# Another offset for a few split weight pages in a stream of three-pass fp32 matmuls

## The chip, the cores and the metric

The kernel runs on one core of one Trainium2 chip. The metric is the device time of one execution in microseconds; of several runs the median is taken.

## What is computed

One layer of a hybrid encoder over 512 tokens of width 2048, all in fp32. Cut to what matters:

```python
h = rms_norm(x, norm_mix_w)
q_a, k_a, v_a, q_g, k_g, v_g, r_g, gate_lr = split(h @ w_in)
y_a = chunked_band_attention(q_a, k_a, v_a, bias)      # 16 heads of 64
o_g = gated_linear_attention(q_g, k_g, v_g, log_a)     # 4 heads
y_g = rms_norm(o_g, gla_norm_w) * silu(r_g)
x = x + concat(y_a, y_g) @ w_out                       # 2048 x 2048
h = rms_norm(x, norm_ffn_w)
u_gate, u_val = split(conv3(h @ w_ffn_up))             # 2048 x 11264
x = x + (gelu(u_gate) * u_val) @ w_ffn_down            # 5632 x 2048
h = rms_norm(x, norm_ple_w)
x = x + sigmoid(h @ w_ple_gate) * (p @ w_ple_proj)     # 2048 x 2048
return rms_norm(x, final_norm_w)
```

## The kernel before

**Products.** The large projections are done by a Strassen-like scheme: a unit is two output blocks of 128 for all 512 tokens, and it is made of seven products (`PLAIN`: P1, P2, P6, P5, P7, P3, P4) of a sum of weight blocks with a prepared combination of the activations. A product is one step. fp32 accuracy comes from splitting each operand into a high and a low part in the matmul's rounded fp32 type: `product` runs three passes over the blocks of 128 of the inner dimension, (high weights, high activations), (high, low), (low, high). With eight blocks (`kb` = 8) a step is 24 matmuls of 128x128 weights with 256 moving columns, with seven blocks 21. The activations are the moving operand; the weight page is the one that is loaded into the array.

**Stages.** The steps lie in one list, `steps`, of 704. `base` says at which step a unit begins. The stages in order: front (16 units: 4 for the linear attention, 8 for the attention, then 4 gate units, 112 steps), the embedding (4 steps of another form), `wo` (8 units, 56 steps), `up` (44 units, 308 steps), `dn0` (8 units, 56 steps, eight blocks), `dn1` and `dn2` (56 steps each, seven blocks), `pg` (56 steps). From `wo` on, the first two and the last two units of a stage are paired: their products alternate, 14 steps for the two.

**Weight pages.** Raw weights come by DMA into pages; some are summed, by a DMA that accumulates (GpSimd's queue) or by VectorE. Two steps before a step's matmuls, `prep_high` has ScalarE write the page's high part (`w<-l` or `w<-s` in the profile) and `prep_low` has VectorE write the low part. Both go into one tile, `w_all`, of 6280 columns: three places for high parts at 0, 1024 and 2048 plus a shift, and three for low parts 3136 columns further on. `weight_pages(shift)` hands them out in rotation, so that step i uses the place of step i-3. In the main loop the shift is 24 columns, so each page starts 96 bytes past a multiple of 256. The tile itself starts at a multiple of 256 in the core's memory, as the compiled program of this kernel places it, and the tiles of the activations (`h`, `wo_R`, `up_N` and the like) start 32 bytes past one; so a page starts 64 bytes further on than its moving operand, modulo 256. For the value projections at the start, where the page is the moving operand and 512 columns are streamed at a time, the shift is 72 (32 bytes past a multiple of 256), and 24 for the last two pages (`value_split`). The last three steps of all put their pages into a free activation tile named `last` (32 bytes past a multiple of 256), as no place of the rotation is free.

**Order.** The order of the engines' work is written out by hand: an `agenda` lists for every step the copies, sums and stores to be issued with it. The three normalisations between stages come as small matmuls in the stage after them (`norm_step`: tile `ms` at the 11th step, `pb` at the 13th).

```python
def weight_pages(shift=72):
    i = counts.get("w", 0)
    counts["w"] = i + 1
    o = i % 3 * 1024 + shift
    return w_all[:, o:o + 1024], w_all[:, 3136 + o:4160 + o]
```

The functions that the change touches:

Of the kernel before, what the change touches and what calls it, by code (L numbers as in the profile page):

```python
# [42 lines left out]
def encoder_block(ctx: ExitStack, tc: tile.TileContext, A, out):  # L43
# [81 lines left out]
# [5 lines that stand above are left out]
# [349 lines left out]
    def make(unit, name):  # L479
        if name not in unit.made:  # L480
            return
        unit.made.discard(name)
        n = unit.stage.kb * P
        w = lambda q: unit.w[q][:, :n]
        if name == "S1":
            vec.tensor_tensor(made_page(unit, "S1")[:, :n], w("L21"), w("L22"), ALU.add)
            used(unit, "L21")
            used(unit, "L22")
            if unit.sums == "s3":
                unit.made.discard("S3")  # L490
                nc.gpsimd.dma_start(w("L21"), w("L11"), accum_op=ALU.add)
                used(unit, "L11")
        elif name == "S2":
            make(unit, "S1")
            vec.tensor_tensor(made_page(unit, "S2")[:, :n], w("S1"), w("L11"), ALU.add)
            used(unit, "S1")
            used(unit, "L11")
        elif name == "S3":
            make(unit, "S1")
            if "S3" in unit.made or unit.sums == "dve":  # L500
                vec.tensor_tensor(w("L21"), w("L21"), w("L11"), ALU.add)
                used(unit, "L11")
        else:
            vec.tensor_tensor(w("S2"), w("S2"), w("L12"), ALU.add)
            used(unit, "L12")

    def prep(i, own=None):
        prep_low(prep_high(i, own))

    def prep_high(i, own=None):  # L510
        if i >= len(steps):
            return None
        unit, prod = steps[i]
        name = PRODUCTS[prod][0]
        n = unit.stage.kb * P
        make(unit, name)
        if prod == unit.order[0] and unit.sums in ("dve", "s3"):
            make(unit, "S1")
        if i + 1 < len(steps):
            nxt, p = steps[i + 1]  # L520
            q = PRODUCTS[p][0]
            if (nxt is unit or nxt.paired) and (q != "S4" or "P6" in nxt.w) and (unit, q) != (front.units[6], "S2"):
                make(nxt, q)
        if i > 0 and steps[i - 1][1] == "P6" and steps[i - 1][0].paired:
            make(steps[i - 1][0], "S4")
        key = name
        if unit.sums != "memory":
            key = {"S4": "S2"}.get(name, "L21" if name == "S3" and unit.sums != "dma" else name)
        raw = unit.w[key]
        hi, lo = own or weight_pages(24)  # L530
        act.activation(hi[:, :n], raw[:, :n], AF.Copy)
        unit.w[prod] = hi, lo
        return unit, key, hi[:, :n], lo[:, :n], raw[:, :n]
# [66 lines left out]
    def load_x(src, unit):  # L600
        unit.xs = page("c", "xs").rearrange("p (s t) -> p s t", s=2)
        nc.sync.dma_start(unit.xs, src[unit.u])
# [56 lines left out]
    def after_norm(dst, xd, col):  # L659
        def after(unit):  # L660
            if unit.last is not None:
                return [(1, 0, lambda: nc.sync.dma_start(dst[unit.u], unit.xs))] + squares(unit, 6 + unit.last * 2)
            return [(0, 1, lambda: residual(dst, unit)), (1, 2, lambda: weighted(col, unit)),
                    (2, 1, lambda: store_pair(xd, unit.u, unit.o[:, 0, :], unit.o[:, 1, :]))] + squares(unit, 3)
        return after
# [46 lines left out]
    def after_gate(unit):  # L712
# [9 lines left out]
    stages = [Stage("wo", list(range(8)), 8, mixd, blk2(A["w_out"]), after_norm(streams[1], h2d, nffn), "s3", "dma", ends=("memory", None),  # L722
                    begin=lambda u: load_x(streams[0], u), begin_at=10, chained=True)]
# [165 lines left out]
    def front_weights(u, q):  # L889
# [4 lines left out]
    front = Stage("in", [12, 13, 14, 15] + list(range(12)), 8, None, front_weights,  # L894
                  lambda u: (attend if u.u < 8 else after_gates if u.u < 12 else linear)(u), "dma",
                  "dma", single=True, late={-4: 6, -12: 3, -11: 2, -10: 1})
# [20 lines left out]
    base = {}  # L917
    for st in stages:
        for group in st.groups:
            base[group[0]] = base[group[-1]] = len(steps)  # L920
            steps += [(u, p) for p in group[0].order for u in group]
            for u in group:
                u.paired = len(group) > 1
            need = [[(u, name) for name in (NEEDS[u.sums] if u.stage is not embed else ("L11",))] for u in group]
            wanted += [e for es in zip(*need) for e in es]

    agenda = [[] for _ in range(len(steps) + 60)]
    now = [0]
    for a, b in zip(stages[2:], stages[3:]):
        i0 = base[a.units[-1]]  # L930
        for n, p in enumerate(PLAIN):
            op = PRODUCTS[p][1]
            for g in range(2):
# [3 lines left out]
                at = 2 * n + (11 if g else 8)  # L937
                k = 3
                if g and b.chained and op in ("R21", "T4"):
                    at, k = max(at, 15), 0 if op == "R21" else 3  # L940
                if b.chained and op == "N1":
                    at = 17 + g
# [109 lines left out]
    for n in range(2):  # L1052
        u = stages[-1].units[n - 2]
        at = end + 4 + n
# [503 lines left out]
    for i, (unit, prod) in enumerate(steps[:-4]):  # L1558
        st = unit.stage
# [7 lines left out]
        if not behind:  # L1567
            coming = prep_high(i + 2) if i < len(steps) - 5 else None
# [3 lines left out]
        if behind:  # L1572
            coming = prep_high(i + 2)
# [112 lines left out]
    lo, hi = lo_half, hi_half  # L1686
# [133 lines left out]
```

## Time and profile before

| | |
|---|---|
| median of 3 runs | 2240.18 us (2231.03 to 2240.95) |
| profiled execution, its own time | 2243.69 us |
| its span, first to last instruction | 2241.9 us |
| mean granted TensorE clock | 0.997 |
| TensorE (PE) busy | 2217.4 us, 18248 matmuls |
| VectorE (DVE) busy | 1895.9 us |
| ScalarE (ACT) busy | 1320.6 us |
| HBM over the span | 273 GB/s |

PE is TensorE's matmuls, PEld its weight loads, which overlap them. A matmul of 256 columns is recorded as lasting about 0.28 us from its first operand to its last result, but the next begins long before it ends; so the busy time of PE says little, and what counts is the time from one start to the next. A stretch of time (a window) lists how many instructions touch it; since a matmul that only reaches into it counts too, a long window has two or three too many.

### The profile page before, as it was taken

What the parts mean: (1) busy time and instruction counts of PE and PEld (TensorE: products, weight loads), DVE (VectorE), ACT (ScalarE), POOL (GpSimd) and SP (SyncE); (2) the same over time, 40 slices, a digit from 0 to 9 for tenths busy, and PEclk for the clock granted to TensorE, in tenths of its full rate; (3) what the DMA queues carried; (4) which work ended last, traced back from release to release, by engine and by line L of the source; (5) the groups of instructions that cost most, each with busy time, mean ns of one, the idle gap of its engine ahead of it and who ended that gap; (6) DMA issues with size and microseconds to landing.
All of it is one profiled execution on the core that took longest, in us unless ns stands there. A gap on an engine that the chain in (4) does not pass through costs nothing.

```text
span 2241.9 us, 45663 instructions
## 1 busy us (share of the span) xinstructions
PE 2217.4 (99%) x18248; PEld 2167.5 (97%) x18248; DVE 1895.9 (85%) x2601; ACT 1320.6 (59%) x1960; POOL 201.0 (9%) x245
## 2 busy tenths in 40 slices
PE   9999999999999999999999999999999999999997
PEld 8879999999899999999999999999999999999997
DVE  6876779997698989898888888888888798898997
ACT  6654567776665765555555545555564564666765
POOL 1021111011100011111111100000000000000000
PEclk9999999999999999999999999999999999999999
DMA  5498889888978979999999987877876967879896
GB/s 206 139 260 246 227 232 250 227 229 236 352 270 250 348 212 286 284 273 288 281 271 275 264 230 207 218 210 193 246 266 221 300 231 231 333 248 333 286 299 207
DMA packets 202340, 569.77 MB, mean 254 GB/s; under 512 B 22064, under 2 KB 64304, under 8 KB 202128
## 3 DMA queue, kind: packets, MB, share of 16 engines
q1 hardware_dynamic: 168336, 448.58, 56.2%
q0 software_dynamic: 32352, 115.88, 27.4%
q8 instruction: 143, 2.34, 0.4%
q10 hardware_dynamic: 1440, 2.40, 0.3%
q14 instruction: 69, 0.57, 0.1%
HBM read 493.37 MB, written 119.54 MB: 273 GB/s over the span
## 4 chain that ended last, share of the span: by engine, by line
PE 81%; DVE 7%; DMA 7%; ACT 2%; issue 2%; SPq 0%; DVEq 0%; POOL 0%; ACTq 0%; POOLq 0%
PE accA L64 41%; PE accC L64 21%; PE accB L64 10%; PE v L64 4%; DVE w L64 2%; DMA on<-ond 1%; DMA s<-in_w_blk 1%; PE pp L64 1%; DMA l<-in_w_ple_gate 1%; DMA wva_s<-in_w_v_a 1%; PE psc L64 1%; PE py L64 1%; PE ptr L64 1%; ACT w L64 1%; DVE u L64 1%
## 5 line engine op out<-in xcount | busy, mean ns | idle before, releaser
L64 PE MATMUL accA<-h,w 128*128 128x256 f32 x5088 | 623.4, 280 | 1.7 <-ACT u L64 1.2
L64 PEld LDWEIGHTS accA<-h,w 128*128 128x128 f32 x5088 | 604.1, 189 | 4.7 <-ACT u L64 2.1
L64 PE MATMUL accC<-h,w 128*128 128x256 f32 x4248 | 520.9, 280 | 3.6 <-DVE w L64 2.6
L64 DVE TENSOR_TENSOR w<-s,w 128x1024 fp32r<-128x1024 f32 (+1 forms) x381 | 457.4, 1201 | 73.7 <-ACT w L64 71.6
L64 PEld LDWEIGHTS accC<-h,w 128*128 128x128 f32 x4248 | 504.9, 189 | 4.5 <-DVE w L64 3.0
L64 ACT ACTIVATE w<-l 128x1024 fp32r<-128x1024 f32 (+1 forms) x320 | 331.7, 1038 | 183.4 <-PE accC L64 119.5
L64 DVE TENSOR_TENSOR w<-l,w 128x1024 fp32r<-128x1024 f32 (+1 forms) x320 | 382.4, 1195 | 58.8 <-ACT w L64 58.6
L64 ACT ACTIVATE w<-s 128x1024 fp32r<-128x1024 f32 (+1 forms) x381 | 394.7, 1037 | 41.2 <-DVE s L64 26.6
L64 ACT ACTIVATE u<-accA 128x256 f32<-128x256 f32 x302 | 114.2, 378 | 376.4 <-PE accA L64 375.7
L64 DVE TENSOR_TENSOR s<-s,l 128x1024 f32<-128x1024 f32 (+1 forms) x176 | 211.3, 1201 | 8.5 <-DMA s<-in_w_blk 8.1
L64 POOL DMA_DIRECT2D s<-in_w_up x84 | 73.9, 880 | 743.8 <-DMA s<-in_w_up 326.2
L64 DVE SCALAR_TENSOR_TENSOR cv<-u,cw,cv 128x511 f32<-128x511 f32 (+1 forms) x176 | 131.6, 748 | 3.1
L64 PE MATMUL accA<-up_R,w 128*128 128x256 f32 x1056 | 131.5, 281 | 0.0
L64 PE MATMUL accB<-up_R,w 128*128 128x256 f32 x1056 | 131.1, 281 | 0.0
L64 PE MATMUL accA<-up_N,w 128*128 128x256 f32 x1056 | 131.1, 281 | 0.0
L64 PEld LDWEIGHTS accA<-up_R,w 128*128 128x128 f32 x1056 | 127.2, 189 | 0.5 <-issue 0.5
L64 PEld LDWEIGHTS accB<-up_R,w 128*128 128x128 f32 x1056 | 127.2, 189 | 0.0
L64 PEld LDWEIGHTS accA<-up_N,w 128*128 128x128 f32 x1056 | 127.1, 189 | 0.0
L64 DVE TENSOR_TENSOR u<-u,accC 128x256 f32<-128x256 f32 x102 | 42.7, 419 | 56.1 <-PE accC L64 55.5
L64 ACT ACTIVATE u<-accC 128x256 f32<-128x256 f32 x98 | 37.3, 381 | 89.5 <-PE accC L64 88.8
L64 PE MATMUL v<-w,h 128*128 128x512 f32 x384 | 88.7, 391 | 0.2 <-ACT h L171 0.2
L64 PEld LDWEIGHTS v<-w,h 128*128 128x128 f32 x384 | 72.1, 188 | 15.8 <-issue 0.5
(302 smaller groups left out, 2884.6 us busy)
## 6 DMA issues: line engine op xcount, KB each, us to landing
l<-in_w_up SPq DMA_DIRECT2D x132, 512.0 KB, 7.0
s<-in_w_up SPq DMA_DIRECT2D x84, 512.0 KB, 5.5
s<-in_w_up POOLq DMA_DIRECT2D x84, 512.0 KB, 7.4
l<-in_w_dn SPq DMA_DIRECT2D x56, 448.0 KB, 5.1
l<-in_w_blk SPq DMA_DIRECT2D x48, 512.0 KB, 5.7
s<-in_w_blk SPq DMA_DIRECT2D x32, 512.0 KB, 4.5
s<-in_w_blk POOLq DMA_DIRECT2D x32, 512.0 KB, 7.7
l<-in_w_out SPq DMA_DIRECT2D x28, 512.0 KB, 5.0
```

The lines of the kernel that those rows point to most:

```text
L64: ins = f(*args, **kw)
```

## The change

A table, `places`, gives fourteen steps a shift of their own, and `prep_high` looks it up; all other steps keep 24. Two steps lie in the gate units (the units of index 13 and 14 of the front), and two in each of the six stages `wo`, `up`, `dn0`, `dn1`, `dn2` and `pg`. They are steps 93 and 99 of the list; then 120 and 132 (`wo`, its steps 4 and 16, counted from 0), 177 and 189 (`up`, 5 and 17), 483 and 498 (`dn0`, 3 and 18), 541 and 553 (`dn1`, 5 and 17), 595 and 610 (`dn2`, 3 and 18), 651 and 666 (`pg`, 3 and 18). In the stages with eight blocks the shift is 36 columns (144 bytes past a multiple of 256); the step is moved on to the next that has the last place of the rotation, so that the page still ends ahead of the first low part. In `dn1` and `dn2` the shift is 0, and the step is moved on to the next that has the first place. A step's page is its high part and its low part, both shifted. Instructions, their order, their sizes and all else stay.

```diff
-        hi, lo = own or weight_pages(24)
+        hi, lo = own or weight_pages(places.get(i, 24))
...
+    places = {}
+
+    def place(i, short):
+        if short:
+            places[i + (1 - i) % 3] = 0
+        else:
+            places[i + -i % 3] = 36
+
+    for unit in (front.units[13], front.units[14]):
+        place(base[unit] + 1, False)
+    for st in stages[2:]:
+        for at in (3, 16):
+            place(base[st.units[0]] + at, st.kb < 8)
```

## The prediction

> **What bounds the kernel now.** I read the page first, then the windows of PE alone, then single steps in the timeline.
>
> ```profile
> span 2241.9 us, 45663 instructions
> PE 2217.4 (99%) x18248; PEld 2167.5 (97%) x18248; DVE 1895.9 (85%) x2601; ACT 1320.6 (59%) x1960; POOL 201.0 (9%) x245
> PE 81%; DVE 7%; DMA 7%; ACT 2%; issue 2%; SPq 0%; DVEq 0%; POOL 0%; ACTq 0%; POOLq 0%
> ```
>
> PE is the bound: it works for 2217.4 of 2241.9 us and makes up 81% of the chain that ended last. The change removes no matmul, so it can win time in only one way, by the time from one matmul's start to the next (its pace). The windows show that this is not one number (us, PE busy and instructions, granted clock, DMA share, GB/s):
>
> ```profile
> 640.00:760.00 120.00, 120.00 (x1062) 1.00 0.85 274
> 820.00:1690.00 870.00, 870.00 (x7389) 1.00 0.89 251
> 1815.00:1970.00 155.00, 155.00 (x1370) 1.00 0.73 254
> 1976.00:2068.00 92.00, 92.00 (x783) 1.00 0.83 296
> 2074.00:2098.00 24.00, 24.00 (x206) 1.00 0.83 281
> 2110.00:2204.00 94.00, 94.00 (x832) 1.00 0.94 293
> 627.00:799.00 172.00, 172.00 (x1519) 1.00 0.85 276
> ```
>
> In all of them PE has no gap and the granted clock is 1.00. Less 2.5 matmuls that only reach in, the paces are 120/1059.5 = 113.3 ns, 870/7386.5 = 117.8, 155/1367.5 = 113.3, 92/780.5 = 117.9, 24/203.5 = 117.9, 94/829.5 = 113.3 and 172/1516.5 = 113.4. So the same 128x256 matmul has two rhythms, a fast one of 113.3 and a slow one of 117.8 ns, 4.5 ns or 3.8% apart, and most of `up` (820 to 1690 us) lies in the slow one. The instructions show it too (ns min/median/max): the weight loads of `accC` in windows 640 to 760 and 1200 to 1300 us, then those from the pages `last` at the end.
>
> ```profile
> L64 PEld LDWEIGHTS accC<-h,w x324: 187/188/188, 641.8 to 760.0; 128*128 128x128 f32 x162
> L64 PEld LDWEIGHTS accC<-h,w x248: 187/188/193, 1199.8 to 1299.6; 128*128 128x128 f32 x124
> L64 PEld LDWEIGHTS accC<-h,last x32: 187/192/193, 2214.6 to 2218.3; 128*128 128x128 f32 x32
> ```
>
> In the fast rhythm no load is late; in the slow one some take 193 ns, which looks like loads and moving reads that meet again and again. What begins and ends a rhythm? Whole steps and breaks from the timeline (start, us from first start to last end, count):
>
> ```profile
> 696.29 2.88 PE L64 MATMUL accA<-wo_N,w 128*128 128x256 f32 x24
> 1200.90 2.99 PE L64 MATMUL accA<-h,w 128*128 128x256 f32 x24
> 798.79 1.07 PE L64 MATMUL accC<-h,w 128*128 128x256 f32 x8
> 800.00 1.05 PE L64 MATMUL ms<-ones,acc 128*128 128x1 f32 x8
> 803.82 2.99 PE L64 MATMUL accA<-h,w 128*128 128x256 f32 x24
> 807.60 3.39 PE L64 MATMUL accA<-up_R,w 128*128 128x256 f32 x24
> 1692.26 1.19 PE L64 MATMUL accA<-h,w 128*128 128x256 f32 x8 [0.30 <-DVE w L64]
> 1973.67 2.74 PE L64 MATMUL accC<-h,w 128*128 128x256 f32 x21 [0.95 <-ACT u L64]
> 2100.90 5.70 PE L64 MATMUL accA<-h,w 128*128 128x256 f32 x48
> 2206.13 3.10 PE L64 MATMUL accA<-h,w 128*128 128x256 f32 x24 [0.39 <-ACT u L64]
> ```
>
> A matmul lasts 0.28 us, so a step's pace is (us - 0.28)/(count - 1): 113.0 ns in the first row, 117.8 in the second, 112.9 before the norm's small matmuls at 800 us and 117.8 right after them. The wait at 1692.26 ends the slow stretch, that at 1973.67 begins another; behind the next norm the pace at 2100.90 is 5.42/47, below 116 with one longer start in it, and the windows on both sides say slow before and fast after; the wait at 2206.13 begins the last slow stretch. Five breaks, three of them to the slow side. In 870 us without a break, over 300 changes of page, of moving tile and of high to low part, the rhythm never changed; it changed at breaks alone, to either side.
>
> **The change part by part.** Fourteen pages lie 48 bytes further on or 96 bytes back; everything else is as it was. What an offset does is seen in two places: in the three last steps, whose page lies 64 bytes nearer to its moving operand, and in the value projections, whose last two pages went from shift 72 to 24 (there the page is the moving operand).
>
> ```profile
> 2214.72 3.52 PE L64 MATMUL accC<-h,last 128*128 128x256 f32 x28
> 167.66 5.60 PE L64 MATMUL vaC<-w,in_R 128*128 128x512 f32 x24
> 173.10 11.12 PE L64 MATMUL vaA<-w,h 128*128 128x512 f32 x48
> ```
>
> The first: (3.52 - 0.28)/27 = 120.0 ns, against 117.8 of the step before it. The second, with a matmul of 0.39 us: 5.21/23 = 226.5 ns; the third has 24 such and then 24 of the new shift, (10.73 - 24 x 0.2265)/23 = 230 ns. So the offset sets the pace at once, in an unbroken stream. I read from it that the pace hangs on how a page's lines and the moving operand's lines fall against each other, that a stream in the odd page takes up the rhythm of that offset, and that it comes back to shift 24 in another phase than it left: a break made without a wait. The trace has no page at 36 or 0.
>
> 1. The odd page itself: its pace lies between 113.3 and 120.0 ns, the fastest and slowest rows. Against a fast stream 14 steps of 24 x 0 to 6.7 ns, so 0 to 2.2 us; I take the middle, 1.1, as neither row is nearer. In the copies on ScalarE and VectorE nothing changes in size.
> 2. `up`, step 189, the one that counts: the third unit begins at 807.60; its first step takes 3.39 - 0.28 + 0.12 = 3.23 us, the next two 24 x 0.1178 = 2.83 each, so its fourth product, the odd page, starts at 816.5 and ends before the window from 820. If the stream leaves that page fast, all to 1690 us is fast: 870 - 7386.5 x 0.1133 = 33.1 us won.
> 3. `pg`, step 651 (about 2075 us): the slow stretch there ends at 2100, by the two rows, so 22 us x 3.8% = 0.8 us.
> 4. `dn2`, step 610: it ends right before the wait at 1973.67, which comes after the odd page and draws anew. I claim nothing; if it fell fast, the 92 us of its window x 3.8% = 3.5 us.
> 5. The other odd pages lie in stretches that are fast already (`wo`, `dn0`, `dn1`, the gate units, step 177, step 666): 0, if a fast stream comes out fast.
> 6. New waits: none. Step i still takes the place of step i-3, 36 columns end the third page at 3108, ahead of 3160, and 0 begins the first at 0, with 896 columns in it.
>
> Can the other engines feed a faster PE? Here with all engines (PE, PEld, DVE, ACT, POOL, clock, DMA share, GB/s):
>
> ```profile
> 820.00:1690.00 870.00, 870.00 (x7389) 870.00 (x7388) 755.85 (x889) 468.93 (x630) 97.46 (x112) 1.00 0.89 251
> 640.00:760.00 120.00, 120.00 (x1062) 120.00 (x1061) 103.52 (x129) 69.46 (x99) 6.93 (x8) 1.00 0.85 274
> 1000.00:1100.00 100.00, 100.00 (x852) 100.00 (x851) 88.18 (x108) 52.25 (x71) 14.86 (x17) 1.00 1.02 286
> L64 ACT ACTIVATE w<-l 128x1024 fp32r<-128x1024 f32 x133 | 140.6, 1057 | 91.2 <-PE accC L64 66.4 <-PE accA L64 21.2 <-DVE l L64 1.8
> ```
>
> VectorE's 755.85 us in 870 become 755.85/837 = 90%; `wo` ran at the fast pace with 86%. The densest part of `up`, 286 GB/s, would ask for 297, and the fast stretch of `pg` had 293 without a gap. ScalarE's wait before the raw pages, 91.2 us in `up`, is nearly all for PE, so the pages are there. I cost the supply at nothing; this slack hides it.
>
> Sum against the profiled execution: 2243.69 - 33.1 - 0.8 + 1.1 = 2210.9 us. It lies 3.5 us above the median of the runs, and I carry the same 32.8 us over: 2240.18 - 32.8 = 2207.4, so 2207.
>
> [...]
>
> **The rivals.**
> *Nothing happens.* The stream comes back into the rhythm it had. For it: 300 page changes in `up` did not disturb it, and `last` is never left again, so no return is shown. Against it: the two jumps above, and the coin that every break throws. Time 2240, to 2242.4 with dear pages. [...]
> *The odd page leaves the stream slow.* Then the stretches that are fast turn slow from the first odd page in each: `wo` and the start of `up` 172 us, `dn0` to `dn2` 1692 to 1973, `pg` 94, in all 547 us x 3.9% = 21 us, and `up` gains nothing: 2240.2 + 21 + 1.1 = 2262, or about 2252 where breaks behind it win half back. It decides at steps 132 and 177: if a stream that was fast leaves them slow. For it: of the five breaks shown three ended slow. Against it: the slow rhythm needs loads that are late again and again, the fast one only that none is.
> *The supply gives way.* A faster `up` runs into one wait midway, the rhythm is drawn anew and falls slow: half of 33 us is lost, 2224. For it: VectorE at 90%. Against it: the slack above.
>
> **How the numbers follow.** Forecast 0.63, nothing happens 0.14, left slow 0.16, supply 0.07. The forecast's own range is 2203 (pages free, `dn2` fast) to 2212. The whole reaches over supply and nothing to 2243 and leaves out the slow case: 2203 to 2243. About 0.5%, 11 us, is what a measurement of this kernel can tell from no change; so faster takes forecast and supply, 0.70, same 0.14, slower 0.16.
>
> **What would show it.** Right: the window 820 to 1650 us holds a step of 24 in 2.88 us, not 2.99, weight loads at most 188 ns, the step behind 816 us already fast, PE without a gap, and `up` ending about 33 us sooner. Wrong: 2.99 us behind the odd page of `up` (nothing happens), 2.99 in `wo` or before 800 us (left slow), or a new wait of PE in `up` (supply). An odd page far above 120 ns would upset term 1.

## The result, and the profile after

Four runs of the changed kernel gave a median of 2213.44 us (2212.25 to 2231.91), four of the kernel before 2240.56 us (2231.03 to 2245.12). The ratio is 0.9897 with a 95% interval of 0.9848 to 0.9945: faster by about 1%, as forecast, 6 us short of the 2207 expected. (The ratio leaves out every run more than 1.5% over its kernel's fastest, here none, but further down up to ten of 19 runs of before, whose granted clock of 0.997 to 0.998 is that of the others, so medians of all runs are given beside it.)

The profiled execution of the changed kernel was the longest of its four, 2231.91 us. Its page:

```profile
span 2230.1 us, 45663 instructions
PE 2205.5 (99%) x18248; PEld 2153.4 (97%) x18248; DVE 1893.2 (85%) x2601; ACT 1322.2 (59%) x1960; POOL 201.3 (9%) x245
PE 79%; DVE 8%; DMA 7%; ACT 3%; issue 2%; SPq 0%; POOL 0%; DVEq 0%; ACTq 0%; POOLq 0%
```

The same instructions, and PE is busy for 11.9 us less: the time is gone from the pace. By stage, from first matmul to first matmul, `up` is 13.1 us shorter (858.9 against 872.0) and `dn2` 3.3 us, while `dn0` is 4.0 us and `pg` 1.8 us longer. Windows of PE (us, PE busy and instructions, clock, DMA share, GB/s):

```profile
820.00:1150.00 330.00, 330.00 (x2914) 1.00 1.01 287
1170.00:1630.00 460.00, 460.00 (x3908) 1.00 0.83 239
1690.00:1790.00 100.00, 100.00 (x851) 1.00 0.80 264
1830.00:1920.00 90.00, 90.00 (x797) 1.00 0.77 270
2110.00:2190.00 80.00, 80.00 (x708) 1.00 0.94 296
```

Less 2.5 matmuls each, the paces are 113.3, 117.8, 117.9, 113.3 and 113.4 ns. `up` was fast from 820 to 1150 us, where it had been slow; then it fell slow after all, and most of `dn0` was slow too (1690 to 1790). The steps around the odd page of `up`, step 189 (start, us, count):

```profile
812.05 2.99 PE L64 MATMUL accA<-up_N,w 128*128 128x256 f32 x24
814.87 3.03 PE L64 MATMUL accC<-h,w 128*128 128x256 f32 x24
817.74 2.90 PE L64 MATMUL accA<-h,w 128*128 128x256 f32 x24
820.48 2.88 PE L64 MATMUL accC<-h,w 128*128 128x256 f32 x24
```

By (us - 0.28)/(count - 1): 117.8 ns before it, 119.6 in it, 113.9 in the step behind (its first matmuls still longer) and 113.0 from then on. What ended the fast stretch, some 340 us later, and what befell `dn0`:

```profile
1149.91 1.23 DVE L64 TENSOR_TENSOR s<-s,l 128x1024 f32<-128x1024 f32 x1 [2.41 <-DMA s<-in_w_up]
1155.28 2.81 PEld L64 LDWEIGHTS accA<-up_N,w 128*128 128x128 f32 x24 [0.28 <-ACT u L64]
1166.30 1.89 PE L64 MATMUL accA<-h,w 128*128 128x256 f32 x14
1674.49 2.08 PE L64 MATMUL accA<-h,w 128*128 128x256 f32 x16
1677.54 1.23 PE L64 MATMUL accA<-h,w 128*128 128x256 f32 x8 [0.96 <-DVE w L64]
1678.60 2.99 PE L64 MATMUL accC<-h,w 128*128 128x256 f32 x24
```

A summed weight page came late (VectorE waited 2.41 us for the accumulating DMA), ScalarE's eviction `u` followed late, and PE's weight loads waited 0.28 us for it, to 1155.28. The stream was fast again from the step behind this first break, a second small one came at 1166 (two starts 133 and 194 ns apart, where 113 to 114 is usual), and behind it all was slow to 1633, where the odd page 483 of `dn0` turned it from 117.8 to 113.3 ns. In `dn0` the odd page itself (step 498, from 1674.49) was cut in two by a wait of PE for its low part; behind the eight matmuls left of it the stream came out slow (2.99). Whether they were too few, or in the wrong phase, is not shown.

### The profile page after: what moved, and what is told of

It reads as the page before. It is cut to its first block, busy times and chain, and to the rows that moved or that the text cites. A ratio compares the mean times of both kernels' runs of the same rounds, so it can differ in the third digit from the quotient of the medians.

```text
span 2230.1 us, 45663 instructions
## 1 busy us (share of the span) xinstructions
PE 2205.5 (99%) x18248; PEld 2153.4 (97%) x18248; DVE 1893.2 (85%) x2601; ACT 1322.2 (59%) x1960; POOL 201.3 (9%) x245
## 4 chain that ended last, share of the span: by engine, by line
PE 79%; DVE 8%; DMA 7%; ACT 3%; issue 2%; SPq 0%; POOL 0%; DVEq 0%; ACTq 0%; POOLq 0%
PE accA L64 40%; PE accC L64 20%; PE accB L64 10%; PE v L64 4%; DVE w L64 3%; DMA s<-in_w_blk 2%; DMA on<-ond 1%; DVE u L64 1%; DVE h L64 1%; PE vaA L64 1%; ACT w L64 1%; DMA s<-in_w_up 1%; DMA l<-in_w_ple_gate 1%; PE py L64 1%; PE psc L64 1%
```

## The experiments

**Without step 189.** The theory was that one page, step 189, carries the gain.

```diff
+    del places[189]
```

> All odd pages of the change except the one at step 189, the fourth product of the third unit of `up`. Theory (an odd page of shift 36 hands a slow stream over to the fast rhythm): `up` falls slow at the norm's break near 800 us, as it did in both profiles, and nothing takes it out; a step of 24 takes 2.99 us from 808 us on, and the time is about 2213 + 33 = 2246 us at worst, 2240 to 2246. Rival (the gain comes from the other thirteen pages, or from breaks that fall otherwise by chance): 2213 to 2220 us. Should the break near 800 us fall fast here, the run says nothing on step 189, and the window 820 to 1600 us tells.

Median 2242.07 us over 10 runs (one of 2215.33, the others 2236.54 to 2247.85) against 2240.8 of before; ratio 1.0035, 0.9986 to 1.0084. Steps 189 and 190, and the window behind:

```profile
814.74 2.99 PE L64 MATMUL accC<-h,w 128*128 128x256 f32 x24
817.57 2.99 PE L64 MATMUL accA<-h,w 128*128 128x256 f32 x24
820.00:1640.00 820.00, 820.00 (x6964) 1.00 0.90 254
```

117.8 ns throughout: the stream entered slow as in the changed kernel, met no odd page and stayed slow for 820 us. Thirteen of the fourteen pages give nothing that can be measured; the one of `up` carries the gain.

**Only step 189.**

```diff
+    places.clear()
+    places[189] = 36
```

> Only step 189 has the odd page, all other steps have shift 24. Theory: `up` is fast from 818 us to about 1690 us, 33 us won against 2240: 2207 to 2212, less or more by the 4 to 5 us that `dn0`, `dn2` and the start of `pg` win or lose at their own breaks. Rival (the pages act together, or the gain is chance): 2225 to 2240. If the break in `up` near 1155 us of the profiled run comes again, the rest of `up` is slow and the time about 2227.

Median 2219.86 us over 10 runs, 2205.51 to 2240.89, against 2240.8 (2206.41 to 2252.93) of before in the same series. The ratio, 1.0001 (0.9951 to 1.005), shows no gain by the rule above; by medians of all runs 21 us of it are there, less than expected. The profiled run, 2231.04 us, shows one way to lose it:

```profile
822.00:1150.00 328.00, 328.00 (x2897) 1.00 1.01 287
1170.00:1670.00 500.00, 500.00 (x4247) 1.00 0.82 235
```

113.3 ns, then 117.8: a gap of 0.7 us between two starts near 1157 us ended the fast stretch, in step 314, where the first break of the changed kernel fell too.

**One odd page after another, each with another shift.**

```diff
+    places.clear()
+    places.update({195: 36, 207: 72, 220: 0, 234: 28, 246: 44, 259: 20, 273: 64, 285: 32, 298: 4,
+                   312: 52, 324: 40, 337: 12, 351: 60, 363: 48, 376: 8, 390: 56, 402: 68, 415: 16})
```

> No page of the change; instead, in `up`, every 12 steps or so one odd page, each with another shift: in order of steps 36, 72, 0, 28, 44, 20, 64, 32, 4, 52, 40, 12, 60, 48, 8, 56, 68, 16 columns. The trace shows the pace inside each page and the rhythm behind it. Theory (the pace hangs on the offset modulo a few lines, and the rhythm behind the page on the phase in which it leaves): inside 36 columns about 119.6 ns and behind it 113.3; inside 0 about 116.7 and behind it 113.3; inside 72 about 120, since that is the offset of the pages named last; the others differ, and some leave the stream slow. Rival (any page off 24 is as good as a break and draws the rhythm anew): the rhythm behind does not go with the offset, and about half of the pages leave it slow. Time between 2207 and 2243.

Four of the pages, each with the step behind it (shifts 36, 72, 0 and 52):

```profile
829.94 3.04 PE L64 MATMUL accA<-up_N,w 128*128 128x256 f32 x24
832.82 2.89 PE L64 MATMUL accC<-h,w 128*128 128x256 f32 x24
862.74 3.04 PE L64 MATMUL accA<-up_R,w 128*128 128x256 f32 x24
865.62 2.99 PE L64 MATMUL accB<-up_R,w 128*128 128x256 f32 x24
899.54 2.97 PE L64 MATMUL accA<-h,w 128*128 128x256 f32 x24
902.35 2.90 PE L64 MATMUL accA<-up_R,w 128*128 128x256 f32 x24
1150.66 2.99 PE L64 MATMUL accA<-up_R,w 128*128 128x256 f32 x24
1153.49 2.99 PE L64 MATMUL accB<-up_R,w 128*128 128x256 f32 x24
```

All eighteen, from the start times of the page's second half; the place is the page's start minus that of its moving operand, in bytes modulo 256:

| place | shift (columns) | ns inside | rhythm before, behind |
|---|---|---|---|
| 0 | 72; 8 | 120.0; 120.0 | fast, slow; fast, slow |
| 16 | 12 | 118.4 | fast, slow |
| 32 | 16 | 118.3 | fast, fast |
| 48 | 20 | 117.8 | fast, fast |
| 80 | 28 | 118.8 | fast, fast |
| 96 | 32 | 120.0 | fast, fast |
| 112 | 36 | 119.4 | fast, fast |
| 128 | 40 | 118.8 | slow, fast |
| 144 | 44 | 120.0 | fast, fast |
| 160 | 48 | 120.0 | fast, fast |
| 176 | 52 | 118.2 | fast, slow |
| 192 | 56 | 117.8 | slow, fast |
| 208 | 60 | 116.7 | slow, fast |
| 224 | 0; 64 | 116.7; 116.7 | slow, fast; fast, fast |
| 240 | 4; 68 | 117.6; 117.6 | fast, fast; fast, fast |

The pace inside a page goes with its place, and repeats at 256 bytes (72 and 8, 0 and 64, 4 and 68). Behind 72, 8, 12 and 52 the stream was slow, behind all others fast. Ten of those fourteen were entered fast, which shows only that they do no harm; 0, 40, 56 and 60 took a slow stream back. The rival, that any odd page is as good as a break, falls: four of eighteen, not half, and the same ones again in the runs below. No place shown is faster than the usual one, 64 bytes, in its fast rhythm.

**Every page at 36.**

```diff
-        hi, lo = own or weight_pages(places.get(i, 24))
+        hi, lo = own or weight_pages(36)
```

> Every page of the main loop at shift 36, none at another. Theory (the pace hangs on the offset, and 36 columns is itself a slow one, 119.6 ns in the pages of the change): every step of 24 takes 2.75 + 0.28 = 3.03 us, PE needs about 16300 x 6.3 ns = 100 us more than all fast, so about 2280 us. Rival (36 is a good offset in itself, and the odd page wins because it is fast): steps of 2.88 us or less everywhere, 2200 us or below.

2296.19 us (two runs), ratio 1.0282 (1.0184 to 1.038); 16 us more than expected, as the expectation counted from 2180. The window:

```profile
820.00:1640.00 820.00, 820.00 (x6830) 1.00 0.88 243
```

820/6827.5 = 120.1 ns. The offset that helps as an exception is a bad one to stay at; the gain is not made in the odd page but behind it.

**The same fourteen steps at the place of the operand.** Shift 72 for 36 and 8 for 0.

```diff
+    places.update({i: 72 if s else 8 for i, s in places.items()})
```

> The fourteen steps of the change with shift 72 in place of 36, and 8 in place of 0. Both put the page at the same place modulo 256 bytes as its moving operand, and the offset run showed 120.0 ns inside them and the slow rhythm behind them. Theory (the offset decides the rhythm behind the page): `wo` from 660 us, `up`, `dn1`, `dn2` and `pg` all slow behind their odd pages, 2.99 us for a step of 24: 2255 to 2265 us, slower than before. Rival (any other offset would do as well as 36): 2207 to 2220.

2259.14 us (two runs), ratio 1.0105 (1.0008 to 1.0201), slower than before. `wo`, `up` and the start of `dn2`:

```profile
662.00:780.00 118.00, 118.00 (x1004) 1.00 0.89 290
825.00:1640.00 815.00, 815.00 (x6922) 1.00 0.90 253
1850.00:1940.00 90.00, 90.00 (x766) 1.00 0.75 252
```

117.8, 117.8 and 117.9 ns, also in `wo`, which is fast in the kernel before. The price of the prediction's rival on the other side, 2262, is 3 us off; it needed another offset.

**The change once more.** Twelve runs beside 17 of before. The code is that of the change.

> The change as it is, once more, to see how its runs spread and as the base of the next two. Theory (the odd page at step 189 always hands over fast; what is left to chance are breaks behind it): most runs between 2207 and 2216 us, and some some 15 to 20 us longer, where a break in the middle of `up` (near 1155 us in two profiles) draws the slow rhythm. Rival (the gain of the first measurement was the luck of four runs): runs spread as those of before, up to 2250.

Median 2218.59 us (2207.87 to 2235.30) against 2236.56 (2217.15 to 2249.95); ratio 0.9927, 0.9883 to 0.9971. Six runs lie between 2207.87 and 2213.83, six between 2223.34 and 2235.30. The profiled one, 2228.03, again breaks in the middle of `up`, this time near 1192 us, where PE waited 0.9 us for `u` of ScalarE, and near 1204:

```profile
820.00:1200.00 380.00, 379.12 (x3346) 1.00 1.01 285
1208.00:1630.00 422.00, 422.00 (x3585) 1.00 0.83 235
```

379.12/3343.5 = 113.4 ns, then 422/3582.5 = 117.8. So the break is no stray of one run: it came in three profiles of three whose `up` was fast from 820 us on with no further odd page.

**Odd pages behind the breaks, and five more in `up`.**

```diff
+    places[501] = places.pop(498)
+    places[613] = places.pop(610)
+    places.update(dict.fromkeys(range(246, 480, 57), 36))
```

> The change with the odd pages of `dn0` and `dn2` moved one rotation on (steps 501 and 613 in place of 498 and 610), so that they lie behind the wait that in the profile falls into or right behind them, and five more odd pages of shift 36 in `up`, every 57 steps from 246 on. Theory: the runs that lose 15 to 20 us are gone, `dn0` is always fast (4 to 5 us in those runs where it was slow): median 2207 to 2211, none over 2220. Rival (breaks take what they take whatever lies behind them): as the change.

2210.68 us, six runs from 2209.14 to 2211.73; ratio 0.9887, 0.9835 to 0.9939. The long runs are gone. Two windows between the pages, 113.3 ns each:

```profile
1130.00:1270.00 140.00, 140.00 (x1238) 1.00 1.01 283
1285.00:1430.00 145.00, 145.00 (x1282) 1.00 0.81 219
```

In this profile `up` lasts 841.6 us from its first matmul to that of `dn0`, against 872.0 before. The first matmuls of the two stages, here and then before (a count is what falls into the window asked for):

```profile
764.17 2.09 PE L64 MATMUL accA<-up_R,w 128*128 128x256 f32 x17
1605.80 0.96 PE L64 MATMUL accA<-dn_R,w 128*128 128x256 f32 x7
767.01 3.22 PE L64 MATMUL accA<-up_R,w 128*128 128x256 f32 x27
1639.03 1.23 PE L64 MATMUL accA<-dn_R,w 128*128 128x256 f32 x9
```

**The moved pages alone** split this kernel.

```diff
+    places[501] = places.pop(498)
+    places[613] = places.pop(610)
```

> The change with the odd pages of `dn0` and `dn2` moved one rotation on (501 and 613), and nothing added in `up`. It splits the kernel with the five more pages in `up` (2209 to 2212 us in all its runs) into its two halves. Theory (long runs come from a break in the middle of `up` behind which nothing takes the stream back): long runs of 2220 to 2235 us stay, in about four of ten, and the short ones are at 2206 to 2211. Rival (the two moved pages did it): all runs at 2209 to 2213.

Median 2210.33 us over 12 runs; eight from 2207.61 to 2213.47, four from 2221.98 to 2240.38. So the long runs are cured by the pages in `up`, as expected. Three of the four, 2239.49 to 2240.38, are longer than the 2235 expected and about as long as the kernel before (2241.53); a step 189 that failed to turn the stream would do that, but none of them was profiled. The profiled run, 2213.47 us, had a break in `up`, near 1192 us, a wait of 0.3 us, that fell fast (679.66/5993.5 = 113.4 ns over the window):

```profile
820.00:1500.00 680.00, 679.66 (x5996) 1.00 0.94 263
1665.68 3.04 PE L64 MATMUL accA<-dn_R,w 128*128 128x256 f32 x24
1668.55 2.99 PE L64 MATMUL accB<-dn_R,w 128*128 128x256 f32 x24
```

And it shows what I had not expected: step 501, at shift 36, entered slow and left slow (2.99 behind it).

**An odd page every 24 steps of `up`, at 64.**

```diff
+    places[501] = places.pop(498)
+    places[613] = places.pop(610)
+    places.update({i: 64 for i in range(210, 480, 24)})
```

> As the last, but in `up` an odd page of shift 64 columns every 24 steps from 210 on (12 pages), which had 116.7 ns inside and the fast rhythm behind it, in place of the five of shift 36. Theory: a slow stretch lasts at most 24 steps, 24 x 24 x 4.5 ns = 2.6 us, and a page costs 24 x 3.4 ns = 0.08 us: median 2206 to 2210, smallest spread. Rival (each odd page costs more than it saves): over the last by 1 us or more.

2209.22 us, six runs from 2205.52 to 2213.22; ratio 0.983 to 0.9935 around 0.9883. The median is as expected; the spread, 7.7 us, is not the smallest, as six runs with five pages had 2.6. Here step 189, at 36, failed to turn the stream (2.99 us in the step behind it); the next odd page is 210, at 64:

```profile
814.72 3.04 PE L64 MATMUL accC<-h,w 128*128 128x256 f32 x24
817.60 2.99 PE L64 MATMUL accA<-h,w 128*128 128x256 f32 x24
```

**Sixteen pairs: into the slow rhythm and out of it.**

```diff
+    places.clear()
+    places.update({198: 72, 204: 36, 213: 52, 219: 36, 226: 12, 234: 36, 241: 8, 249: 36, 258: 72, 264: 64,
+                   273: 52, 279: 64, 286: 12, 294: 64, 301: 8, 309: 64, 318: 72, 325: 0, 333: 52, 340: 0,
+                   349: 12, 355: 0, 364: 8, 370: 0, 378: 72, 384: 40, 393: 52, 399: 40, 406: 12, 414: 40,
+                   421: 8, 429: 40})
```

> No page of the change; in `up` sixteen pairs: a page that has left the stream slow (shift 72, 52, 12 or 8), and 5 to 10 steps behind it one that should take it back: four times each shift 36, 64, 0 and 40. Theory (by phase): 64 and 0, the same place modulo 256, take all eight slow streams to 113.3; 36 may fail where it is entered in another phase, as it did once; 40 is open. Rival (a page's shift alone settles what is behind it): 36 takes all four back too, and the one failure was a stray. Time 2215 to 2235.

All sixteen pages at 72, 52, 12 and 8 left the stream slow. 64 and 0 took it back eight times of eight, 36 four of four, 40 two of four. Steps 384 and 399, both at 40 and both entered slow, each with the step behind:

```profile
1359.28 3.01 PE L64 MATMUL accA<-up_N,w 128*128 128x256 f32 x24
1362.12 2.99 PE L64 MATMUL accC<-h,w 128*128 128x256 f32 x24
1401.71 3.01 PE L64 MATMUL accC<-h,w 128*128 128x256 f32 x24
1404.56 2.89 PE L64 MATMUL accA<-h,w 128*128 128x256 f32 x24
```

The same shift, another outcome, so the shift alone does not settle it. The start times tell the two apart inside the page: the last five intervals are 121, 120, 119, 115 and 118 ns in step 384, and 120, 119, 115, 117 and 122 in step 399, the same cycle left one matmul later. The two pages at 40 that failed (384 and 429) stand behind pages of 72 and 8, place 0; the two that did not (399 and 414) behind 52 and 12. The rival falls, though not by the page I had named for it. The time, 2244.03, was 9 us over my range, as `dn0`, `dn1` and `pg` fell slow with no odd page behind their breaks.

**Only 64 and 0.**

```diff
+    places[501] = places.pop(498)
+    places[613] = places.pop(610)
+    places.update({i: 64 if s else 0 for i, s in places.items()})
+    places.update({i: 64 for i in range(213, 480, 24)})
```

> The kernel with an odd page every 24 steps of `up` and the ones of `dn0` and `dn2` behind the wait, but every odd page of shift 36 (119.6 ns inside) now at 64 (116.7 ns inside), and the twelve of `up` at 213, 237 and on. In the run before, step 189 at shift 36, entered from the slow rhythm, left the stream slow once. Theory (the rhythm behind a page hangs on the phase in which it is left; at 64 the inside rhythm has a period of four matmuls, at 36 of five): 64 takes every slow stream to the fast one, no stretch of `up` longer than 24 steps is slow, median 2205 to 2209, no run over 2213. Rival (36 and 64 are the same): as the run before, 2209 with runs to 2213.

2210.35 us, twelve runs from 2206.64 to 2213.14, against 2239.81 of before; ratio 0.9934 (0.9896 to 0.9971). The median is 1 us over the forecast and the longest run at its bound, nearer to the rival's 2209 with runs to 2213; by time 36 and 64 can't be told apart once there are enough pages.

```profile
820.00:1600.00 780.00, 780.00 (x6877) 1.00 0.92 261
```

780/6874.5 = 113.5 ns with its odd pages. Over all profiles, pages without a break in or right behind them that were entered slow: at 36 fourteen of sixteen left fast, at 64 and 0 seventeen of seventeen. Entered fast, 36 left fast 39 times of 39.

**The operand moved, not the page.** In the kernel before, the filler tile ahead of the activation tiles made 64 bytes shorter, so that R11, R21 and N2 stand at the place of the pages.

```diff
-    shim = ...tile([P, 112], F32, tag="shim", name="shim")
+    shim = ...tile([P, 96], F32, tag="shim", name="shim")
```

> The kernel before, every page at shift 24, but the filler tile ahead of the activation tiles is 96 columns instead of 112, which moves the operands R11, R21 and N2 of every stage (three of seven steps) 64 bytes on, so that they stand at the same place modulo 256 as the pages; the operands in `h` stay. Theory (what counts is the page's place against that of its moving operand): steps on `up_R` and `up_N` take 120.0 ns a matmul, as the pages of shift 72 and 8 did, and those on `h` behind them fall slow, 117.8: about 2265 to 2275 us. Rival (the page's own offset counts, whatever it meets): 113.3 or 117.8 ns everywhere as before, 2207 to 2250 us.

2243.33 us (one run), 22 us under the range expected.

```profile
1201.19 3.02 PE L64 MATMUL accA<-up_R,w 128*128 128x256 f32 x24
1204.06 3.04 PE L64 MATMUL accB<-up_R,w 128*128 128x256 f32 x24
1206.94 3.04 PE L64 MATMUL accA<-up_N,w 128*128 128x256 f32 x24
1209.82 2.90 PE L64 MATMUL accC<-h,w 128*128 128x256 f32 x24
1212.56 2.88 PE L64 MATMUL accA<-h,w 128*128 128x256 f32 x24
```

120.0 ns on the moved operands, with every page where it was: it is the place of the page against its operand that sets the pace. But behind them the steps on `h` were fast (2.90 and 2.88 us), not slow as I had expected. A place of 0 left by changing the operand comes out otherwise than one left by changing the page, which fits a phase, and not the place alone; that it is the phase is not shown here.

## Why the prediction was right, and where it was not

**What bounds the kernel** held: the same instructions, and all of the gain in the time from one start to the next. **Term 2**, the odd page of `up`, held in mechanism and size: removing it alone took the gain away, and where `up` stayed fast to its end it was 872.0 - 841.6 = 30.4 us shorter. Of the 33.1 forecast, 1.9 lay in the first 50 us of `dn0`, and these were not won: in that profile `dn0` took 154.8 us, against 154.9. "A break made without a wait" was too loose: behind a break the stream came out to either side (behind the wait in step 611, 113.4 ns from 1966 to 2050 us in the first profile of the change, against 117.9 in the kernel before), behind an odd page of one offset nearly always to the same side. The odd page's outcome goes by the offset and, as the two pages at 40 and their cycles suggest, by the phase in which the slow stream enters it. That loads and moving reads meet, line against line, was my reading of loads of 193 ns against 188, and no run shows it; the runs show the pace by the place of the page against its operand, 113.3 to 120.0 ns, the same for places 256 bytes apart.

**The step that failed** is "I cost the supply at nothing; this slack hides it". Six of the twelve runs of the change took 2223.34 to 2235.30 us, the others at most 2213.83. The two profiles of the change are both of long runs, and in both a break in the middle of `up` lost the fast rhythm; the first of them names a late accumulated page, in a stretch with a DMA share of 1.01 and 287 GB/s. The rival with that mechanism had been priced at 2224, near the long runs' 2223 to 2235, but given 0.07. The window I had argued from, 293 GB/s without a gap in `pg`, was 94 us long; `up` held 287 GB/s for 330 us before it broke. Why the page is late, and why the break came in all four profiles whose `up` was fast without further odd pages (in step 314 or 328) and in none with them, was not settled: the three kernels with more pages show no two starts over 135 ns apart in `up` behind step 186, so that a page caught a break there was not seen, only that long runs vanished (none of 24 over 2213.3 us). The first four runs were also lucky: one of them was long, and six of the next twelve, whose median of 2218.59 is 12 us over the forecast.

**Term 1**, the odd page, measured 119.6 ns at 36 and 116.7 at 0: ten steps of 24 x 6.3 ns and four of 21 x 3.4 make 1.8 us, not 1.1. **Term 3**, 0.8 us in `pg`, did not show: step 651 turned the stream fast (113.3 ns behind it), but `pg` took 178.4 us to the end, against 176.6 before, with longer waits in it (1.2 us for `u` of ScalarE against 0.4, and 0.5 us for `w` of VectorE against none). **Term 4** was as said: what is behind the wait after step 610 can fall to either side, 113.4 ns in the first profile of the change and 117.9 in the kernel before. **Term 5** missed that a wait could fall into an odd page: `dn0` took 158.9 us instead of 154.9 in the first profile. A dearer page, 0.7 us, and `dn0`, 4.0 us, would be most of the 6 us between 2207 and 2213; as no run of 2213 us of the change was profiled, where they lie is not shown.

**The rivals.** "Nothing happens" falls with the first two experiments; the pace went from 113.3 to 120.0 ns with the place of a page alone (shift 72 in a fast stream). "Left slow" is true of shifts 72, 52, 12 and 8, and false of 36 and 0: no stream that entered these fast left them slow, and of sixteen that entered 36 slow two stayed so.

## What to carry to other kernels

Where matmuls run back to back and the granted clock is full, count starts per window: two paces of the same instruction, here 113.3 and 117.8 ns, were moved in this kernel by how weight page and moving operand lie against each other, and the offset of one tile against the other is then worth a sweep. In this kernel a rhythm that held for hundreds of microseconds was chosen at the last break or odd page, so one page at another offset behind each break was worth more (2210.68 us, against 2236.56 of before) than the same offset for all pages (2296.19 against 2240.8). The kernel to keep is one with such a page behind every known break and some more in the long stretch: 2209 to 2211 us, with no long runs, against 2218.59 for the change in twelve runs.

## What the runs showed of the hardware

At a granted clock of 1.00 a 128x256 fp32r matmul stream ran at 113.3 ns or at 116.7 to 120.0 ns a matmul, by the start of the weight page against that of the moving operand modulo 256 bytes (fifteen multiples of 16 bytes in the table, and 64 bytes as the usual place). At 64 bytes two rhythms are stable, 113.3 and 117.8 ns; in the slow one every step of 24 took 2.99 us for over 800 us on end. Places of 112 and 224 bytes led from either into the fast one, 112 from the slow one 14 times of 16 and 224 all 17 times; places of 0, 16 and 176 bytes led into the slow one with all 20 pages at shifts 72, 52, 12 and 8 in the run of one odd page after another and in that of the pairs.
